# The first triple of each group sends its 264-column product ahead of the 272-column one

## The chip, the cores and the metric

The kernel runs on one core of one Trainium2 chip. The metric is the device time of one launch in microseconds (us), the median over runs. The engines are named as the profile names them: PE is TensorE (matrix products, with their weight loads as a stream of their own, PEld), DVE is VectorE, ACT is ScalarE, POOL is GpSimd and SP is SyncE, which issues the transfers.

## The reference, cut to what matters

One inference step of a one-layer hybrid decoder trunk. There are 264 tokens: 256 of a prompt and 8 of decode samples, each with 2048 features, all in float32.

```python
xn = rms_norm(x, g_mix)
z  = xn @ w_in                                   # 2048 -> 3584, split among three mixers
y_pool = pool_mixer(...) @ w_pool_br             #  512 -> 2048
y_lru  = (rg_lru(...) * gelu(u_gel)) @ w_lru_br  # 1024 -> 2048
y_conf = conformer(...) @ w_conf_br              #  512 -> 2048
gates  = sigmoid(xn @ w_gate + b_gate)           # 2048 -> 3 * 2048
x = x + (g_a*y_pool + g_b*y_lru + g_c*y_conf) @ w_out
hid = square(relu(rms_norm(x, g_mlp) @ w_up))    # 2048 -> 8192
x = x + hid @ w_down                             # 8192 -> 2048
y = rms_norm(x, g_final)
```

The states of the pooling, of the two convolutions and of the recurrence are outputs too. Nearly all of the work is the product of 264 tokens with weights that are read once.

## The kernel before, in words

*Three products for one.* TensorE takes float32 data rounded to a shorter form (fp32r), so each operand is split in a high part, the rounded value, and a low part, the rest. A product of x and w becomes hi(w)·hi(x) + lo(w)·hi(x) + hi(w)·lo(x), added up in PSUM. Here these three products are called a triple. On the activation side `high(t, k)` and `low(t, k)` lie next to each other in one row, low first: columns 0 to 263 are low, 264 to 527 are high, and in each the 256 prompt tokens come before the 8 samples. N is 264, TP is 256 and TS is 8.

*Two forms of a triple.* A form is three entries (low weights?, first column, last column). ALIKE sends three times 264 columns: high with whi, high with wlo, low with whi. MIXED sends 272, 264 and 256 columns: first the low part of the 8 samples together with the whole high part with whi (columns 256 to 527), then high with wlo, then low of the 256 prompt tokens with whi. The 8 sample columns of the first product go to their own place at the start of the PSUM bank (`ps[:, :8]`), and `join` or `add_side` adds them to the sample's columns when a group is evacuated. Both forms send 792 columns.

*Groups, chunks and order.* `weight_plan` (line 66) lists 67 groups, each one block of 512 output columns: 7 of w_in, 12 of w_gate, 4 each of w_pool_br, w_lru_br, w_conf_br and w_out, and 16 each of w_up and w_down. A group is cut into chunks, each with two rows of 128 weights (kt = 0, 1) and 512 columns, which are four tiles of 128 (m = 0 to 3). A chunk of 1024 columns is thus 8 triples, 24 products. A group of 2048 inputs has 8 chunks, one of 512 has 2. Each of the four tiles m adds up in its own PSUM bank (`acc`), and there are 8 banks, so two groups' worth. The first group (gi = 0) sends ALIKE, its first four chunks by operand and not by triple; all later groups send MIXED. Between them stand 4 chunks of the RG-LRU gates and one of the pooling's grouped map with 12 products of 264 columns each, and four single products with `ones_r` (line 323) for sums over features.

*What feeds TensorE.* SyncE reads the weights in the order of the plan into `raw`. For each chunk `split` (line 214) makes ScalarE round `raw` to `whi` (line 221), and VectorE subtract that from `raw` into `wlo` (line 222), three chunks ahead of the one that TensorE works on. The order on every queue is the order in which the program is written. `tile_mm` calls `mm3`, which calls `mm` (line 240) three times: every product of the three parts is recorded at line 243. The product that opens a bank has `start=True`. The evacuation of a group follows its last chunk, on VectorE for the most part, with background work of the mixers spread over the chunks by a table of costs (`run_bg`).

Of the kernel before, what the change touches and what calls it, by code (L numbers as in the profile page):

```python
# [91 lines left out]
def hybrid_step(ctx: ExitStack, tc: tile.TileContext, first, par_in, st_in, wall, y_out, st_out):  # L92
# [28 lines left out]
    def pv(name, i=None, n=1):  # L121
        a, b = PCOL[name]
        return par[:, a:b] if i is None else par[:, a + i:a + i + n]
# [26 lines left out]
    def acc():  # L150
        return psum.tile([P, 512], F32, name="acc", tag="acc")

    def tokens(ps):
        return ps[:, TS:TS + N]
# [22 lines left out]
    def dma_pair(p):  # L177
        s = (2 * p) % NRAW
        if p >= n_pairs:
            return  # L180
        if 2 * p >= SINGLE and chunks[2 * p][3] == chunks[2 * p + 1][3] == CH:
            nc.sync.dma_start(raw[:, s:s + 2, :], wall[p - FIRST // 2].rearrange("p (a c) -> p a c", a=2))
        else:
            for h in range(2):
                if chunks[2 * p + h][3]:
                    dma_part(2 * p + h, 0, chunks[2 * p + h][3])
# [27 lines left out]
    def split(j, half=None):  # L214
        if j >= len(chunks) or not chunks[j][3]:
            return
        r, h, lo = raw[:, j % NRAW, :], whi[:, j % NHI, :], wlo[:, j % NHI, :]
        s = slice(0, chunks[j][3])
        if half is not None:
            s = slice(half * 512, half * 512 + 512)  # L220
        nc.scalar.copy(h[:, s], r[:, s])  # L221
        nc.vector.tensor_tensor(lo[:, s], r[:, s], f(h[:, s]), op=ALU.subtract)  # L222
# [13 lines left out]

    ALIKE = (False, N, 2 * N), (True, N, 2 * N), (False, 0, N)
    MIXED = (False, TP, 2 * N), (True, N, 2 * N), (False, 0, TP)

    def mm(ps, hi, lo, x, what, start, stop=False):  # L240
        low_w, a, b = what
        o = TS + N - (b - a) if b > N else TS
        nc.tensor.matmul(ps[:, o:o + b - a], lo if low_w else hi, x[:, a:b], start=start, stop=stop,  # L243
                         skip_group_check=True)
# [119 lines left out]
    def x_tile(k):  # L364
        x_high(k)
        x_low(k)
# [31 lines left out]
    def softplus():  # L398
        sc = G[:, 8, :]
        t0, t1, t2, w, t4 = (sc[:, 8 * i:8 * i + 8] for i in range(5))  # L400
        lam = pv("lru_lambda")
        nc.scalar.activation(t0, lam, AF.Abs)
        nc.scalar.activation(w, t0, AF.Exp, scale=-1.0)
        nc.vector.tensor_scalar(t0, w, 2.0, None, op0=ALU.add)
        nc.vector.reciprocal(t1, t0)
        nc.vector.tensor_scalar(t4, lam, -1.0, 0.0, op0=ALU.mult, op1=ALU.max)
        eng = nc.gpsimd
        eng.tensor_tensor(t0, w, t1, op=ALU.mult)
        eng.tensor_tensor(t1, t0, t0, op=ALU.mult)
        terms = 10  # L410
        eng.memset(t2, 2.0 / (2 * terms + 1))
        for i in range(terms - 1, -1, -1):
            eng.tensor_tensor(t2, t2, t1, op=ALU.mult)
            eng.tensor_scalar(t2, t2, 1.0, 2.0 / (2 * i + 1), op0=ALU.mult, op1=ALU.add)
        eng.tensor_tensor(t2, t2, t0, op=ALU.mult)
        eng.tensor_tensor(t2, t2, t4, op=ALU.add)
        eng.tensor_scalar(sp[:, 0:8], t2, 4.0, 0.0, op0=ALU.mult, op1=ALU.add)
        eng.tensor_scalar(sp[:, 8:16], t2, -8.0, 0.0, op0=ALU.mult, op1=ALU.add)


    def small(at, n):
        return st[:, at - S_SMALL:at - S_SMALL + n]
# [7 lines left out]
    def state_move(i, move):  # L430
        move(tails[i], slice(i * TAIL, (i + 1) * TAIL))
# [481 lines left out]
    def group(gi):  # L913
        name, k0, _, m = groups[gi]
        if name == "w_in":
            def rhs(i):
                return both(a_all, i)
            fn = {0: pool_evac, 1: lru_x_copy, 2: lambda c, p: lru_x_evac(4 + c, p), 3: gel_evac,
                  4: lambda c, p: gel_evac(4 + c, p), 5: ca_evac, 6: cb_evac}[m]
            return rhs, fn  # L920
        if name == "w_gate":
            return (lambda i: both(a_all, i)), (lambda c, p: gate_evac(m // 4, m % 4, c, p))
        if name == "w_pool_br":
            assert "grp" in done
            return (lambda i: both(Q(), i)), (lambda c, p: branch_evac(0, m, c, p))
        if name == "w_lru_br":
            assert "lru" in done
            return (lambda i: both(LH(), i)), (lambda c, p: branch_evac(1, m, c, p))
        if name == "w_conf_br":
            assert "conf" in done  # L930
            return (lambda i: both(Q(), 4 + i)), (lambda c, p: branch_evac(2, m, c, p))
        if name == "w_out":
            return (lambda i: both(a_all, i)), (lambda c, p: out_evac(m * 4 + c, p))
        if name == "w_up":
            return (lambda i: both(*bpart(i))), (lambda c, p: up_evac(m // 4, (m % 4) * 4 + c, p))
        q = k0 // 16
        return (lambda i: both(*hid(q, i))), (lambda c, p: down_evac(q, m * 4 + c, p))
# [31 lines left out]

    def tile_mm(i, c, kt, m, rhs, pss, stop, form=MIXED):  # L970
        s = slice(kt * 512 + m * P, kt * 512 + (m + 1) * P)
        mm3(pss[m], whi[:, i % NHI, s], wlo[:, i % NHI, s], rhs(2 * c + kt), c == 0 and kt == 0, stop,
            form)
# [17 lines left out]
    for i, ch in enumerate(chunks):  # L991
        now[0] = i
        if i < 5:
            x_tile(2 * i + 6)
            x_tile(2 * i + 7)
        for half in (0, 1) if i < 2 else (None,):
            split(i + AHEAD, half)
        if i == 12:
            softplus()
            again = first[:, KD:KD + 4 * HEAD].rearrange("p (k c) -> p k c", k=4)[:, :, :N]  # L1000
            nc.sync.dma_start(X[:, 0:4, :], again)
            nc.vector.tensor_scalar(gfin, pv("g_final"), -0.5, None, op0=ALU.mult)
        if i % 2 == 0:
            dma_pair((i + 8) // 2)
        if i == 2:
            nc.sync.dma_start(par, par_in)
            nc.sync.dma_start(small(S_SMALL, S_IN - S_SMALL), st_in[:, S_SMALL:])
        if 13 <= i < 17:
            state_move(i - 13, lambda t, s: nc.sync.dma_start(t, st_in[:, s]))
        kind, gi, c, _ = ch  # L1010
        if kind == "dense":
            rhs, fn = group(gi)
            name = groups[gi][0]
            n = groups[gi][2] // 2
            if c == 0:
                pss = [acc() for _ in range(4)]
            if i < len(chunks) - 2:
                for kt in range(2):
                    if i < LEAD:
                        by_operand(i, kt, rhs, pss)  # L1020
                    for m in range(4 * (i < LEAD), 4):
                        tile_mm(i, c, kt, m, rhs, pss, c == n - 1 and kt == 1,
                                    MIXED if gi else ALIKE)
            elif i == len(chunks) - 1:
                for m in range(4):
                    for b in range(4):
                        tile_mm(i - 1 + b // 2, c - 1 + b // 2, b % 2, m, rhs, pss, b == 3)
            if c == n - 1:
                for m in range(4):
                    if (gi, m) == (len(groups) - 1, 3):  # L1030
                        last_evac(pss[m])
                    else:
                        if gi and name not in ("w_out", "w_down"):
                            join(pss[m], name in ("w_in", "w_conf_br"))
                        fn(m, pss[m] if name in ("w_out", "w_down") else tokens(pss[m]))
                after(gi)
        elif kind == "lru":
            for j in range(2):
                lru_gate_mm(2 * gi + j, i, j)
            if gi == 3:  # L1040
                lru_tail()
        elif kind == "grp":
            grp_mm(i)
        if i == len(chunks) - 4:
            nc.scalar.preload_act_table_set(ROOT)
        if 136 <= i < 140:
            state_move(i - 136, lambda t, s: nc.sync.dma_start(st_out[:, s], t))
        if i == 140:
            nc.sync.dma_start(st_out[:, S_SMALL:], st)
        if 5 <= i < 9:  # L1050
            x_squares(i - 5)
        if i == 9:
            later(0, x_sum)
        if i == 12:
            later(0, x_rms)
        run_bg()
# [148 lines left out]
```

## Time and profile before

| | |
|---|---|
| time, median of 3 runs | 1374.05 us (1373.83 to 1377.09) |
| the profiled execution | 1374.28 us, its span 1372.5 us |
| mean granted TensorE clock | 0.997 |
| busy: PE, DVE, ACT, POOL | 99%, 65%, 53%, 7% |
| instructions of PE | 11421 products, as many weight loads |
| read from device memory | 252.57 MB, 186 GB/s over the span |

How to read the rows that follow. A row of a group of instructions has line, engine, operation, output and inputs, shape and count, then the busy time and the mean duration in ns of one. Products are pipelined, and the ends that the profile gives them are modelled: one is shown as some 280 ns long while the next one starts about 119 ns later. So the pace of TensorE is read from starts, not from durations. A row of the timeline has start and length in us, and merges neighbours of the same name: a row with x2 is two products, the second of which started inside it. In such a row here, whi x2 is the last product of a triple and the first of the next, shown with the form of the first one. Each triple has one product with `wlo`, which has a row of its own.

### The profile page before, as it was taken

To read this page: it belongs to the slowest core of one execution; us is meant where nothing else is said; L and a number is where in the kernel's file an instruction comes from. 1 tells how busy PE (TensorE), PEld (TensorE's weight loads), DVE (VectorE), ACT (ScalarE), POOL (GpSimd) and SP (SyncE) were. 2 spreads that over 40 slices of the span, in tenths; PEclk is the share of its full clock that TensorE was granted. 3 is DMA by queue.
4 is the path that set the end of the run, shared out by engine and by line. 5 is a ranking of instruction groups with operands and counts; after the bars stand their busy time and mean duration, and the time that the engine had idled before them with its cause. 6 is when DMAs were issued, how large, how long until landed. Compare 5 with 4: busy or idle time off the path is not lost.

```text
span 1372.5 us, 26899 instructions
## 1 busy us (share of the span) xinstructions
PE 1362.0 (99%) x11421; PEld 1360.0 (99%) x11421; DVE 892.5 (65%) x1460; ACT 727.3 (53%) x1061; POOL 97.6 (7%) x125
## 2 busy tenths in 40 slices
PE   9999999999999999999999999999999999999997
PEld 9999999999999999999999999999999999999997
DVE  7686888876877669666656455655465645465544
ACT  7667677666664646455544334543344533354544
POOL 0230010110102014010000000000000000000013
PEclk9999999999999999999999999999999999999998
DMA  8655556555565555555555555555555555555552
GB/s 324 208 179 200 175 192 197 185 181 188 185 212 188 183 187 181 187 181 185 189 183 185 185 185 185 186 186 183 187 186 184 186 187 184 187 185 185 187 184 77
DMA packets 40824, 257.51 MB, mean 188 GB/s; under 512 B 4480, under 2 KB 6784, under 8 KB 11776
## 3 DMA queue, kind: packets, MB, share of 16 engines
q1 hardware_dynamic: 40272, 255.19, 54.8%
q8 instruction: 89, 1.46, 0.4%
q10 hardware_dynamic: 432, 0.61, 0.1%
q14 instruction: 31, 0.25, 0.1%
HBM read 252.57 MB, written 3.21 MB: 186 GB/s over the span
## 4 chain that ended last, share of the span: by engine, by line
PE 99%; DVE 0%; DMA 0%; ACT 0%; DVEq 0%; issue 0%
PE acc L243 99%; DMA tmp<-first_dram 0%; DVE y L1091 0%; DVE acc L1082 0%; DVEq L1182 0%; DVE G L1081 0%; DVE acc L1080 0%; PE acc L1068 0%; PE acc L323 0%; ACT whi L231 0%; ACT rstd L1075 0%; DVE G L892 0%; DVE X L889 0%; DVEq L1082 0%
## 5 line engine op out<-in xcount | busy, mean ns | idle before, releaser
L222 DVE TENSOR_TENSOR wlo<-raw,whi 128x1024 fp32r<-128x1024 f32 (+1 forms) x478 | 581.8, 1219 | 440.3 <-ACT whi L221 439.6
L221 ACT CAST whi<-raw 128x1024 fp32r<-128x1024 f32 (+1 forms) x478 | 496.9, 1042 | 569.8 <-PE acc L243 500.5
L243 PE MATMUL acc<-A,whi 128*128 128x256 f32 (+2 forms) x3968 | 709.3, 281 | 0.2 <-ACT whi L231 0.2
L243 PEld LDWEIGHTS acc<-A,whi 128*128 128x128 f32 x3968 | 609.4, 188 | 0.8 <-ACT whi L231 0.6
L243 PE MATMUL acc<-A,wlo 128*128 128x264 f32 x1984 | 555.3, 282 | 0.0
L243 PEld LDWEIGHTS acc<-A,wlo 128*128 128x128 f32 x1984 | 370.9, 188 | 0.0
L243 PE MATMUL acc<-xn,whi 128*128 128x272 f32 (+1 forms) x2048 | 366.0, 281 | 0.0
L243 PEld LDWEIGHTS acc<-xn,whi 128*128 128x128 f32 x2048 | 314.7, 188 | 0.0
L243 PE MATMUL acc<-xn,wlo 128*128 128x264 f32 x1024 | 288.5, 282 | 0.0
L243 PEld LDWEIGHTS acc<-xn,wlo 128*128 128x128 f32 x1024 | 192.2, 188 | 0.0
L243 PE MATMUL acc<-Q,whi 128*128 128x256 f32 (+2 forms) x776 | 140.7, 281 | 0.0
L243 PE MATMUL acc<-LH,whi 128*128 128x272 f32 (+1 forms) x768 | 138.9, 281 | 0.0
L243 PEld LDWEIGHTS acc<-Q,whi 128*128 128x128 f32 x776 | 120.1, 188 | 0.0
L243 PEld LDWEIGHTS acc<-LH,whi 128*128 128x128 f32 x768 | 118.7, 188 | 0.0
L243 PE MATMUL acc<-Q,wlo 128*128 128x264 f32 x388 | 109.3, 282 | 0.0
L243 PE MATMUL acc<-LH,wlo 128*128 128x264 f32 x384 | 108.2, 282 | 0.0
L860 POOL TENSOR_TENSOR G<-G 128x264 f32<-128x264 f32 x28 | 27.1, 968 | 789.0 <-ACT G L858 788.1
L243 PEld LDWEIGHTS acc<-Q,wlo 128*128 128x128 f32 x388 | 72.8, 188 | 0.0
L243 PEld LDWEIGHTS acc<-LH,wlo 128*128 128x128 f32 x384 | 72.1, 188 | 0.0
L640 ACT ACTIVATE G<-tmp,par 128x256 f32<-128x256 f32 x120 | 54.3, 500 | 7.9 <-DVE G L643 7.1
L643 DVE TENSOR_TENSOR G<-G 128x1024 f32<-128x1024 f32 x30 | 38.2, 1274 | 0.0
L899 DVE TENSOR_TENSOR X<-X,acc 128x264 f32<-128x264 f32 x79 | 33.4, 422 | 6.4 <-PE acc L243 6.4
(185 smaller groups left out, 591.3 us busy)
## 6 DMA issues: line engine op xcount, KB each, us to landing
raw<-wall_dram SPq DMA_DIRECT2D x226, 1024.0 KB, 4.9
raw<-wall_dram SPq DMA_DIRECT2D x12, 512.0 KB, 6.1
raw<-first_dram SPq DMA_DIRECT2D x6, 512.0 KB, 8.1
X<-first_dram SPq DMA_DIRECT2D x6, 264.0 KB, 7.7
raw<-wall_dram SPq DMA_DIRECT2D x5, 256.0 KB, 3.0
tmp<-first_dram SPq DMA_DIRECT2D x3, 388.0 KB, 4.5
y_dram<-y SPq DMA_DIRECT2D x3, 264.0 KB, 2.2
tmp<-st_dram SPq DMA_DIRECT2D x4, 188.0 KB, 5.1
```

The costliest lines, as they stand in the source:

```text
L221: nc.scalar.copy(h[:, s], r[:, s])
L222: nc.vector.tensor_tensor(lo[:, s], r[:, s], f(h[:, s]), op=ALU.subtract)
L243: nc.tensor.matmul(ps[:, o:o + b - a], lo if low_w else hi, x[:, a:b], start=start, stop=stop, skip_group_check=True)
L640: nc.scalar.activation(dst[:, ct, :TP], vext[:, ct, k:k + TP], AF.Copy, scale=par[:, w:w + 1])
L643: nc.vector.tensor_tensor(VC[:, :, :TP], VC[:, :, :TP], src[:, :, :TP], op=ALU.add)
L860: nc.gpsimd.tensor_tensor(sq2, sq2, t, op=ALU.add)
L899: nc.vector.tensor_tensor(X[:, m, :], X[:, m, :], tokens(whole), op=ALU.add)
```

## The change

In the first triple of every group but the first one (c = 0, kt = 0, m = 0), the first two products change places: high with wlo, 264 columns, opens the bank, and the 272-column product comes second. The third stays. The triples of the group's other three tiles, which open their banks as well, and all later triples keep the order 272, 264, 256.

```diff
     ALIKE = (False, N, 2 * N), (True, N, 2 * N), (False, 0, N)
     MIXED = (False, TP, 2 * N), (True, N, 2 * N), (False, 0, TP)
+    OPENING = MIXED[1], MIXED[0], MIXED[2]
...
                     for m in range(4 * (i < LEAD), 4):
                         tile_mm(i, c, kt, m, rhs, pss, c == n - 1 and kt == 1,
-                                    MIXED if gi else ALIKE)
+                                    ALIKE if not gi else MIXED if c or kt or m else OPENING)
```

## The prediction

> **What bounds the kernel now.** I read the page first (busy shares, chain), then the waits of TensorE, then the chain in order of time, then TensorE's groups with the forms kept apart, and last the timeline at single places.
>
> ```profile
> span 1372.5 us, 26899 instructions
> PE 1362.0 (99%) x11421; PEld 1360.0 (99%) x11421; DVE 892.5 (65%) x1460; ACT 727.3 (53%) x1061; POOL 97.6 (7%) x125
> PE acc L340 <- PEq L1176: 0.8, 1, 0.8
> PE acc L1068 <- DVE G L892: 0.3, 1, 0.3
> PE acc L243 <- ACT whi L231: 0.2, 1, 0.2
> 43.55 392.54 PE acc L243 x3300
> 436.21 22.83 PE acc L243 x192
> 459.17 85.63 PE acc L243 x720
> 647.93 713.35 PE acc L243 x6000
> ```
>
> The three rows with an arrow are all the waits of TensorE that this view has: 1.3 us in 1372.5. The last four are pieces of the chain that ended last (start, length, what, how many): it is nothing but the products of line 243, and the longest piece runs 6000 of them back to back. 713.35 / 6000 = 0.11889 us for a product, 0.3567 us for a triple of 272, 264 and 256 columns. So the kernel's time is the number of products times the pace at which TensorE takes them, and a change can act through a wait before a product, or through the pace. The piece of 6000 runs over 31 group boundaries without a break.
>
> The pace is not a property of the columns alone. Here are the rows of the products by form in three stretches (minimum, median and maximum ns of one, first and last start), single rows of TensorE's timeline, and three stretches from the windows, whose third figure from the end is the granted clock:
>
> ```profile
> L243 PE MATMUL acc<-A,wlo x34: 281/281/283, 16.8 to 28.4; 128*128 128x264 f32 x34
> L243 PE MATMUL acc<-A,whi x80: 283/285/288, 28.5 to 42.9; 128*128 128x272 f32 x40, 128*128 128x256 f32 x39, 128*128 128x264 f32 x1
> L243 PE MATMUL acc<-A,wlo x40: 281/286/286, 28.4 to 42.7; 128*128 128x264 f32 x40
> L243 PE MATMUL acc<-A,whi x456: 275/281/287, 547.8 to 629.0; 128*128 128x272 f32 x76, 128*128 128x256 f32 x76
> L243 PE MATMUL acc<-A,wlo x228: 281/282/283, 547.9 to 628.9; 128*128 128x264 f32 x114
> ...
> 16.83 0.40 PE L243 MATMUL acc<-A,wlo 128*128 128x264 f32 x2
> 17.20 0.28 PE L243 MATMUL acc<-A,wlo 128*128 128x264 f32 x1
> 28.36 0.28 PE L243 MATMUL acc<-A,wlo 128*128 128x264 f32 x1
> 28.72 0.29 PE L243 MATMUL acc<-A,wlo 128*128 128x264 f32 x1
> 42.65 0.29 PE L243 MATMUL acc<-A,wlo 128*128 128x264 f32 x1
> 43.26 0.29 PE L323 MATMUL acc<-L,ones_r 128*128 128x264 f32 x1
> 43.51 0.28 PE L243 MATMUL acc<-A,wlo 128*128 128x264 f32 x1
> 547.89 0.28 PE L243 MATMUL acc<-A,wlo 128*128 128x264 f32 x1
> 628.86 0.28 PE L243 MATMUL acc<-A,wlo 128*128 128x264 f32 x1
> ...
> 28.60:42.90 14.30, 14.30 (x120) 14.30 (x119) 12.45 (x17) 8.18 (x11) 0.00 (x0) 1.00 0.59 200
> 548.00:629.00 81.00, 81.00 (x684) 81.00 (x683) 50.37 (x73) 38.77 (x53) 9.29 (x11) 1.00 0.55 184
> 17.10:28.50 11.40, 11.40 (x98) 11.40 (x97) 8.48 (x11) 9.83 (x13) 0.00 (x0) 1.00 1.03 398
> ```
>
> There is one wlo product in each triple, so the step between them is the time of a triple.
> - Three times 264 columns (the first group): from 17.20 to 28.36 are 31 steps, 0.3600 us.
> - 272, 264, 256 in w_out: from 547.89 to 628.86 are 227 steps, 0.3567 us. I call this the quick pace.
> - The same 272, 264, 256 directly behind the first group: from 28.72 to 42.65 are 38 steps, 0.3666 us. The wlo product's median is 286 ns here against 282. I call this the slow pace. It held until one product of other operands, the ones product at 43.26, came in between.
>
> All three add up to 792 columns, with the granted clock at 1.00 in each. So the stream of weight loads and products locks into one pace or another, by what came before, and stays there. This is the only thing in the profile through which an exchange of two neighbouring products can be worth more than itself.
>
> **The change part by part.** The list of instructions that the changed kernel builds, against that of before, differs in 66 places on TensorE: in the first triple of each of the 66 groups behind the first, the 264-column product with wlo now stands ahead of the 272-column product with whi. VectorE, ScalarE, GpSimd and SyncE issue the same instructions in the same order with the same waits. Nothing is added or removed: as many products, weight loads, columns and PSUM writes as before.
>
> *The wait that moves.* The wlo product waits for VectorE's subtraction and now stands one product, 0.12 us, earlier; behind it, in TensorE's queue, is the whole stream. The group with the least slack opens at 97.6, the usual one has that of 721.96:
>
> ```profile
> 95.28 1.22 DVE L222 TENSOR_TENSOR wlo<-raw,whi 128x1024 fp32r<-128x1024 f32 x1
> 97.72 0.28 PE L243 MATMUL acc<-A,wlo 128*128 128x264 f32 x1
> 714.68 1.22 DVE L222 TENSOR_TENSOR wlo<-raw,whi 128x1024 fp32r<-128x1024 f32 x1 [1.63 <-ACT whi L221]
> 721.96 0.28 PE L243 MATMUL acc<-A,whi 128*128 128x272 f32 x1
> 722.08 0.28 PE L243 MATMUL acc<-A,wlo 128*128 128x264 f32 x1
> ```
>
> The residue is ready at 95.28 + 1.22 = 96.50 and at 715.90, 1.22 and 6.18 us ahead of the product that reads it. Moving it 0.12 us up leaves 1.1 us at the tightest place, so this costs 0; the cover is the three chunks by which the splits run ahead. If the cover were gone everywhere, it would cost one product per group, 66 × 0.12 = 7.9 us. The whi product is now wanted later, which frees nothing: no opening waited for it. The last product of the triple, and with it each release of a weight buffer or of PSUM, keeps its place, so no cast, split, evacuation or transfer is started at another time.
>
> *The order itself.* Before has a 264 behind a 256 only where products of other operands come in, and never a 256 behind a 272, so the direct cost has to be bounded. Nearest are the chain's pieces. Behind a ones product: 22.83 − 64 × 0.3567 = 0.00 us over a piece of 64 triples, and 85.63 − 240 × 0.3567 = 0.02 us over one of 240. The piece of 3300 has five blocks of 264-column products in it, 60 products in all (the four lru gate blocks and one grouped map of 12 each; the rows of whi stand in the last fence, x32 and x8, and each has half as many of wlo): 392.54 − 1080 × 0.3567 − 20 × 0.3600 = 0.1 us, 0.02 for each block. That is what it costs to throw the stream out of step once and let it find the quick pace again. On the other side an opening could be a little shorter: neighbouring starts in the timeline lie 0.11 to 0.13 us apart, so 0.01 us is what one product could win. Per opening −0.01 to +0.03 us, over 66: −0.7 to +2.0 us. I take +0.01, the middle of the two pieces behind a ones product, since one product out of place is nearest to what an exchange does: +0.7 us.
>
> *The sum.* The profiled execution took 1374.28 us (a span of 1372.5 and 1.8 around it): 1374.28 + 0 + 0.7 = 1375.0. The median of the runs, 1374.05, is 0.2 lower, so I forecast 1374.8 us, with 1373.3 to 1376.1 as this case's own range. Faster or slower by 0.3% (4.1 us) is about what a measurement of this kernel can tell from no change.
>
> [...]
>
> **The rivals.**
>
> *Slower: an opening throws the stream into the slow pace, and it stays.* Price: 0.3666 − 0.3567 = 0.0099 us a triple. The triples are those of
>
> ```profile
> L243 PE MATMUL acc<-A,whi 128*128 128x272 f32 x1920 | 547.4, 285 | 0.0
> L243 PE MATMUL acc<-xn,whi 128*128 128x272 f32 x1024 | 291.8, 285 | 0.0
> L243 PE MATMUL acc<-Q,whi 128*128 128x272 f32 x384 | 109.4, 285 | 0.0
> L243 PE MATMUL acc<-LH,whi 128*128 128x272 f32 x384 | 109.4, 285 | 0.0
> ...
> L243 PE MATMUL acc<-L,whi 128*128 128x264 f32 x32 | 6.5, 284 | 0.0
> L243 PE MATMUL acc<-Q,whi 128*128 128x264 f32 x8 | 1.6, 284 | 0.0
> ```
>
> The first four rows make 1920 + 1024 + 384 + 384 = 3712, of which 40 are slow already. All the others: 3672 × 0.0099 = 36 us, 1411 us; half of them (one opening locks it, the next unlocks it): 1392 us. It decides over the sign as soon as 4.1 / 0.0099 = 414 triples, 11%, go slow. For it: the pace exists, held 39 triples with no wait behind it, and began at a group opening. Against it: in the rest of the trace the stream was disturbed ten times (four blocks of lru gates, one grouped map, four ones products, that at 43.26 among them, and one short stall in w_out) and each time it came to the quick pace, at the prices worked out above.
>
> *Faster: an opening finds a quicker pace than any seen.* The three paces lie 3.3 ns (360.0 − 356.7) and twice that (366.6 − 360.0) apart. One such step below the quick one, an estimate from these rows, is 353.4 ns: 3712 × 0.0033 = 12 us, 1362 us. For it: the paces do come in steps, and nothing shows that the quick one is the lowest. Against it: no stretch of 1372 us shows it.
>
> *The wlo wait takes over:* 1374.3 + 7.9 = 1382 us at most. The slack of 1.1 us at the tightest opening speaks against it.
>
> That the change doesn't do what it says is out: the built list shows the 66 exchanges.
>
> **How the numbers follow.** Eleven times the stream was thrown out of step: once it locked slow. The same opening recurs, so its outcome is not averaged over 66 tries but repeats for a kind of boundary. With five kinds (A to A, into Q, into LH, back to A, into xn2), each with 10 in 11 for quick, all stay quick with (10/11)^5 = 0.62, so slow 0.38. A quicker pace was met 0 times in 11; I give it 0.20 all the same, since none of the eleven was an exchange of lengths. The wait gets 0.01, and no change keeps 0.41. Faster 0.20, same 0.41, slower 0.39. The range reaches over the slow case, down to 1371 for the spread of the runs, up to 1411; it leaves out the quicker pace and little else.
>
> **What would show it.** Right: TensorE's chain in pieces of 0.1189 us a product, the wlo product's median at 282 ns after the openings, no new wait on VectorE's wlo, 1.3 us of TensorE waits. Slow pace: wlo steps of 0.3666, whi products with a minimum of 283 instead of 275, the span longer with TensorE still at 99% and no wait. Quicker pace: wlo steps under 0.3567 and a shorter span. Moved wait: TensorE waiting on L222 at group starts. What would make me wrong is that I cannot compute which pace an opening leads to; I only count.

## The result, and the profile after

The changed kernel took 1390.76 us (median of 4 runs, 1390.45 to 1391.04) against 1375.57 us (1373.83 to 1377.34) for the kernel before beside it: a ratio of 1.011, with a 95% interval of 1.0093 to 1.0128. It is slower by some 15 us. That is not the forecast of 1374.8 us; it lies within 1.3 us of the rival's second sum, the slow pace in half of the triples (1392 us). Two of the four runs of the kernel before are some 3 us longer than the other two (1377.09 and 1377.34 against 1373.83 and 1374.05); against the two shorter ones the loss is 16.8 us.

The profiled execution took 1390.54 us. Here are the span and the busy shares from its page, all waits of TensorE, and the pieces of the chain that ended last (start, length, what, count):

```profile
span 1388.8 us, 26900 instructions
PE 1378.3 (99%) x11421; PEld 1376.5 (99%) x11421; DVE 892.4 (64%) x1460; ACT 725.8 (52%) x1061; POOL 97.3 (7%) x125
...
PE acc L341 <- PEq L1177: 0.8, 1, 0.8
PE acc L1069 <- DVE G L893: 0.3, 1, 0.3
PE acc L244 <- ACT whi L231: 0.2, 1, 0.2
...
42.87 397.64 PE acc L244 x3300
440.63 22.84 PE acc L244 x192
463.59 190.70 PE acc L244 x1584
654.42 723.16 PE acc L244 x6000
```

The span is 16.3 us longer (1388.8 against 1372.5). Nothing waits more: the three waits are the same 1.3 us as before, TensorE is at 99% again, and the same 6000 products that took 713.35 us now take 723.16, in one piece without a break. The whole loss is pace. (The line that records the products is 244 now; it was 243.)

Two neighbouring groups of w_up show it. First the products of group 37 by form, then those of group 38 (minimum, median and maximum ns of one, first and last start), then rows of TensorE's timeline at the openings of the groups 36 to 40 (start, length):

```profile
L244 PE MATMUL acc<-xn,whi x128: 279/285/288, 682.7 to 705.9; 128*128 128x256 f32 x64, 128*128 128x272 f32 x64
L244 PE MATMUL acc<-xn,wlo x64: 282/286/286, 682.8 to 706.0; 128*128 128x264 f32 x64
...
L244 PE MATMUL acc<-xn,whi x128: 275/283/288, 706.1 to 728.7; 128*128 128x256 f32 x64, 128*128 128x272 f32 x64
L244 PE MATMUL acc<-xn,wlo x64: 281/282/292, 706.3 to 728.9; 128*128 128x264 f32 x64
...
659.86 0.28 PE L244 MATMUL acc<-xn,whi 128*128 128x256 f32 x1
659.97 0.28 PE L244 MATMUL acc<-xn,wlo 128*128 128x264 f32 x1
682.68 0.28 PE L244 MATMUL acc<-xn,whi 128*128 128x256 f32 x1
682.80 0.28 PE L244 MATMUL acc<-xn,wlo 128*128 128x264 f32 x1
706.14 0.28 PE L244 MATMUL acc<-xn,whi 128*128 128x256 f32 x1
706.26 0.29 PE L244 MATMUL acc<-xn,wlo 128*128 128x264 f32 x1
729.11 0.28 PE L244 MATMUL acc<-A,wlo 128*128 128x264 f32 x1
752.57 0.29 PE L244 MATMUL acc<-A,wlo 128*128 128x264 f32 x1
```

The wlo medians of 286 and 282 ns are those of the slow and the quick pace in the prediction. From opening to opening, group 36 takes 22.83 us, group 37 23.46, group 38 22.85, group 39 23.46: 64 triples at 0.3567 or at 0.3666. So one opening locks the slow pace, and the next one unlocks it.

Over the whole trace, with each of the 3712 triples taken from its own first start to the next product's, 1653 run slow (365 to 369 ns) and 1957 quick (356 to 360), where before it was 42 and 3658. (1653 − 42) × 0.0099 = 15.9 us of the 16.3. Most of the rest lies at the openings: the triples that are neither went from 12 to 102.

**What decides an opening.** In the quick stream the triples are not all alike. The time from the start of a triple's 256-column product to the start of what follows is 112 or 113 ns in one triple and 117 or 118 in the next, and so on in turn (113, 117, 113, 118 ns ahead of the opening at 682.80); in the slow stream it is 119 or 120 in every triple. Sorted by that time in front of the exchanged triple, from the starts in ns (all openings behind the first one that is exchanged):

```
pace before -> behind   openings   gap behind the 256-column product
quick -> quick              4      113 ns (4)
quick -> slow              31      117 ns (13), 118 ns (18)
slow  -> quick             30      119 ns (23), 120 ns (7)
```

There is no exception. An exchange behind a short gap keeps the quick pace; behind a long gap it locks the slow one; in the slow stream it releases it. In the rows above it is 0.11 at 659.86 (stays quick), 0.12 at 682.68 (locks); these rows are rounded to 0.01 us, and a single one does not always show it. A group has an even number of triples, so the alternation comes through a whole group in step. This was read from the same trace that it explains, so it had to be tested.

### The profile page after: what moved, and what is told of

The parts are those of the page before. It is cut to its first block, busy times and chain, and to the rows that moved or that the text cites. A ratio compares the mean times of both kernels' runs of the same rounds, so it can differ in the third digit from the quotient of the medians.

```text
span 1388.8 us, 26900 instructions
## 1 busy us (share of the span) xinstructions
PE 1378.3 (99%) x11421; PEld 1376.5 (99%) x11421; DVE 892.4 (64%) x1460; ACT 725.8 (52%) x1061; POOL 97.3 (7%) x125
## 4 chain that ended last, share of the span: by engine, by line
PE 99%; DVE 0%; DMA 0%; ACT 0%; DVEq 0%; issue 0%
PE acc L244 99%; DMA tmp<-first_dram 0%; DVE y L1092 0%; DVE acc L1083 0%; DVEq L1183 0%; DVE G L1082 0%; DVE acc L1081 0%; PE acc L1069 0%; PE acc L324 0%; ACT whi L231 0%; ACT rstd L1076 0%; DVE G L893 0%; DVE X L890 0%; DVEq L1083 0%
## 5 line engine op out<-in xcount | busy, mean ns | idle before, releaser
L244 PE MATMUL acc<-xn,whi 128*128 128x272 f32 (+1 forms) x2048 | 370.1, 283 | 0.0
```

## The experiments

All the runs below are compared with runs of the kernel before on the same chip, 1373.95 us (19 runs), 1374.22 (13) or 1374.12 (21) in the median.

### One, two and three exchanges

The exchange is made at group 37 alone, at 37 and 38, and at 37, 38 and 39. If each exchange had its own price, two would cost twice what one does. By the alternation, one costs nothing but shifts the step, the second locks the pace for all 29 groups that follow, and the third releases it.

```diff
-ALIKE if not gi else MIXED if c or kt or m else OPENING)
+ALIKE if not gi else OPENING if gi == 37 and not (c or kt or m) else MIXED)               # one
+ALIKE if not gi else OPENING if gi in (37, 38) and not (c or kt or m) else MIXED)         # two
+ALIKE if not gi else OPENING if gi in (37, 38, 39) and not (c or kt or m) else MIXED)     # three
```

> The exchange in one group alone, group 37 (the third of w_up), all others as before. Theory of the lock: in the quick stream the triples come in two kinds that alternate, seen in the gap behind the 256-column product (112 to 113 ns, then 117 to 118). In the changed kernel an exchange behind a triple with the 117 to 118 ns gap led to the slow pace, one behind the 112 to 113 ns gap kept the quick one and shifted the alternation by one triple. In the kernel before, group 37 opens behind a short gap, so here nothing locks: no more than 0.1 us slower than before. Rival, a toll: each exchange costs its share of what 66 cost, 15.2 / 66 = 0.23 us. Rival, any exchange in the quick stream locks slow: the 1920 triples from there to the end at 9.9 ns, +19 us.

> The exchange in groups 37 and 38 alone. Theory of the lock: the first shifts the alternation, so that the second falls behind the long gap and locks the stream slow; no exchange follows to set it free, and nothing else comes in between until the end: 29 groups with 64 triples at 9.9 ns, +18.4 us, about 1392.5 us. Two exchanges would then cost more than the 66 of the changed kernel. Toll: 2 x 0.23 = 0.5 us.

> The exchange in groups 37, 38 and 39 alone. Theory of the lock: shift, lock, release; only the 64 triples of group 38 are slow, +0.6 us, and the rest of the chain has the pace of before. Toll: 3 x 0.23 = 0.7 us, so the time doesn't tell these two apart, but the trace does: 64 slow triples in group 38 and none behind it.

One: 1373.82 us, ratio 1.0 (0.9991 to 1.0009). Two: 1393.9 us, 1.0143 (1.0126 to 1.016). Three: 1374.85 us, 1.0 (0.9987 to 1.0013). The last piece of the chain and the openings in the timeline; of one:

```profile
647.45 713.38 PE acc L244 x6000
675.74 0.28 PE L244 MATMUL acc<-xn,whi 128*128 128x256 f32 x1
675.85 0.28 PE L244 MATMUL acc<-xn,wlo 128*128 128x264 f32 x1
```

of two:

```profile
647.76 731.91 PE acc L244 x6000
676.02 0.28 PE L244 MATMUL acc<-xn,whi 128*128 128x256 f32 x1
676.13 0.28 PE L244 MATMUL acc<-xn,wlo 128*128 128x264 f32 x1
698.85 0.28 PE L244 MATMUL acc<-xn,whi 128*128 128x256 f32 x1
698.97 0.28 PE L244 MATMUL acc<-xn,wlo 128*128 128x264 f32 x1
```

and of three:

```profile
544.99 105.84 PE acc L244 x864
650.82 0.12 PE acc L324
650.95 714.01 PE acc L244 x6000
```

The exchange at 37 stands behind a gap of 0.11 and changes nothing (713.38 against 713.35); that at 38, behind 0.12, costs 731.91 − 713.38 = 18.5 us (29 groups × 64 triples × 0.0099 = 18.4), although it exchanges just two products; the third leaves group 38 alone slow, 0.63 us. Two exchanges cost more than 66, and three cost next to nothing. No price for each exchange can do that; a pace that an opening locks and the next one unlocks does.

Three shows something else besides. Its profiled run was one of 1377.92 us. The kernel before, too, has runs of 1376 to 1377.3 us beside those of 1373 to 1375, 14 of 57 in this study, and one more of 1379.36. In the row at 544.99, 864 products behind the short stall in w_out took 105.84 us, where the profile of before has

```profile
544.83 102.97 PE acc L243 x864
```

The difference is 2.87 us, and 288 triples × 0.0099 are 2.85. The pace locked slow behind the stall, and the ones product at 650.82 released it. No exchange lies in that stretch. The stall is in the profile of before too, and there the stream came out of it quick.

The slow stretch behind the first group is no fixed one either. In the profiles of before, one and two its 39 triples are slow; in that of three they are quick from the third on, though group 1 is sent alike in all four.

### The exchange in the middle of a group

An opening also starts a PSUM bank and a group. Here the two exchanges are made in the fifth chunk of the groups 37 and 38, where neither starts.

```diff
-ALIKE if not gi else MIXED if c or kt or m else OPENING)
+ALIKE if not gi else OPENING if gi in (37, 38) and (c, kt, m) == (4, 0, 0) else MIXED)
```

> The exchange in groups 37 and 38 again, but in the first triple of their fifth chunk and not in the first triple of the group: there the product that comes first opens no bank, it adds to what is there. Theory of the lock: where in a group it stands doesn't matter; the fifth chunk starts an even number of triples (32) behind the group's start, so as with the exchanges at the openings the second locks: 1856 - 32 = 1824 triples, +18.1 us. Rival, the opening of a bank with 264 columns in place of 272 is what disturbs: no effect, 1374 us.

1393.43 us, ratio 1.0135 (1.0113 to 1.0157). The last piece of the chain is

```profile
647.45 731.59 PE acc L244 x6000
```

18.2 us over that of one, 0.3 less than in two, which is the half group that now comes ahead of the lock. The opening as such has no part in it.

### Columns or weights

The exchange moves two things: 264 columns come ahead of 272, and wlo comes ahead of whi. In the first kernel only the columns change places and whi stays first; in the second only the weights do.

```diff
-    OPENING = MIXED[1], MIXED[0], MIXED[2]
+    OPENING = (False, N, 2 * N), (True, TP, 2 * N), (False, 0, TP)      # lengths alone
+    OPENING = (True, TP, 2 * N), (False, N, 2 * N), (False, 0, TP)      # weights alone
-ALIKE if not gi else MIXED if c or kt or m else OPENING)
+ALIKE if not gi else OPENING if gi in (37, 38) and not (c or kt or m) else MIXED)
```

> In the opening triples of groups 37 and 38 only the columns are exchanged, not the weights: 264 columns with whi, 272 with wlo, 256 with whi (the low part of the 8 sample columns is thus multiplied with the low weights there, and its product with the high weights is left out). If the lengths and places of the columns make the lock, the same as the two exchanges: +18 us, about 1393 us, slow from group 38 on. If it is the order of the weights, no change, 1374 us.

> The counterpart: in the opening triples of groups 37 and 38 the weights are exchanged, not the columns: 272 columns with wlo, 264 with whi, 256 with whi (the same part left out). If the columns make the lock: no change, 1374 us, the last piece of the chain 713.4 us as before. If the order of the weights does: +18 us.

Lengths alone: 1392.57 us, ratio 1.0132 (1.0112 to 1.0152). Weights alone: 1373.75 us, 0.9997 (0.9987 to 1.0007). The last pieces, of lengths alone and then of weights alone:

```profile
648.09 731.91 PE acc L244 x6000
```

```profile
647.35 713.35 PE acc L244 x6000
```

The exchange of the columns alone gives the whole effect, 731.91 us as in two. The test of the weights is weaker than it looks. Their exchange at 37 did not shift the alternation, so that at 38 also fell behind a short gap (113 and 112 ns in front of the two), where even the whole exchange locks nothing. It shows that the weights alone do not shift the step; an exchange of weights alone behind a long gap was not run. The columns have a length and a place of their own (each product reads another part of the row of activations), and these two were not told apart.

### The new order in every triple

```diff
-ALIKE if not gi else MIXED if c or kt or m else OPENING)
+ALIKE if not gi else OPENING if True else MIXED)
```

> All triples behind the first group send 264, 272, 256 columns, not the openings alone. The three products then follow each other in the one other order that a cycle of three has. Theory of the lock: no opening shifts the alternation any more, so the pace is one and the same over long pieces, whichever it is: 1374 us if this order can run at 356.7 ns a triple, 1411 us if it runs at 366.6 throughout; a value between them, with groups in turn quick and slow as in the changed kernel, would be against it. I have nothing that tells which; a toll for each exchange would give 3712 x 0.23 = 854 us more.

1410.15 us, ratio 1.0259 (1.0242 to 1.0277); the last piece is

```profile
663.91 733.20 PE acc L244 x6000
```

733.20 / 2000 = 0.3666 us for a triple: the slow pace. The order 264, 272, 256 showed no quick stretch in this run. The 16 triples of the last two chunks are sent by a line of their own and keep the old order; the last 12 of them are back at 0.3567. The prediction's upper end, every triple slow at 1411 us, is what this kernel runs at.

### The place of the activations in a row

If the pace hangs on how three reads of a row follow each other, it may hang on where they start. Each row of a stored activation begins at the column `k * PITCH + SKEW`, with `SKEW = 56`; 4 columns are 16 bytes. The kernel before is moved as a whole.

```diff
-SKEW = 56
+SKEW = 64      # and 60, and 72
```

> The kernel before with SKEW 64 in place of 56: every row of the activations' two parts starts 32 bytes later, so that the low part starts at a multiple of 64 bytes in place of the high part. The products' lengths and order are those of before. If the paces are a matter of the lengths alone, 1374 us. If they are a matter of where the columns lie, the piece of 6000 products leaves its 713.4 us; whether up or down I can't say.

> The kernel before with SKEW 60 in place of 56: all rows of the activations start 16 bytes later. With 64 (32 bytes later) the stream ran at 360.0 and 373.3 ns a triple in place of 356.7 and 366.6. If what counts is the place within 64 bytes, this is a third set of paces; if only the step of 32 bytes counts, one of the two known ones. The last piece of 6000 products tells: 713.4 us at 356.7 ns, 720.0 at 360.0.

> The kernel before with SKEW 72, 64 bytes later than 56: the same place within 64 bytes, another one within 128. If the place within 64 bytes makes the paces, all is as before: 713.4 us for the last 6000 products, 1374 us. If a longer period counts, another pace.

With 60: 1396.69 us, ratio 1.0163 (1.0144 to 1.0181). With 72: 1397.72 us, 1.017 (1.0152 to 1.0189). With 64: 1394.68 in the run with the profile and 1417.40 to 1418.34 in the three others, so no ratio is given. The last pieces for 60, 64 and 72, each from its own chain:

```profile
656.77 726.68 PE acc L243 x6000
```

```profile
661.69 720.02 PE acc L243 x6000
```

```profile
658.04 726.68 PE acc L243 x6000
```

That is 0.3633, 0.3600 and 0.3633 us a triple, where 56 has 0.3567. Not one product, weight or column is exchanged here, and the pace moves by up to 1.9%. If the place within 64 bytes made the pace, 72 would run like 56; it does not, and that reading fell.

The kernel with 64 has two paces as well. Of an earlier piece of 64 triples its profile says

```profile
443.57 23.88 PE acc L243 x192
```

That is 0.3731 us a triple, against 0.3600 in the last piece. What took the three longer runs of 64 to 1418 us was not profiled; a long stretch in the slower of these paces would be a way, and is not shown.

### Without the stall, and the best of both

The locking behind the stall in w_out (three, above) can be taken away at its cause. The two background steps that cast and subtract an operand of w_out were two chunks apart; here the subtraction comes one chunk earlier. The second kernel adds the exchange at group 1 alone: in the changed kernel the slow pace that follows the first group, 39 triples in the profile of before, ended after 3.

```diff
-            later_split(A(k), A(16 + k), t, 3, 2)
+            later_split(A(k), A(16 + k), t, 3, 1)
# best, in addition:
-ALIKE if not gi else MIXED if c or kt or m else OPENING)
+ALIKE if not gi else OPENING if gi == 1 and not (c or kt or m) else MIXED)
```

> The kernel before, with the low parts of the merged branches split one chunk earlier on VectorE (gap 1 in place of 2 in later_split), so that the third chunk of w_out finds them ready. In the profile of the run with three exchanges the same short stall in w_out was followed by the slow pace up to the ones product at 650, and its piece of 864 products took 105.84 us in place of 102.97. Theory of the lock: with the stall gone the stream stays quick there in every run, the piece takes 864 / 3 x 0.3567 = 102.7 us, and the runs at 1376 to 1377.5 us that the kernel before has beside those at 1374 are gone: all at 1373.3 to 1374.3. Rival, the stall only costs itself: 0.25 us less in every run, and the two kinds of run stay.

> The same, and the exchange at the opening of the second group (group 1) alone, where the kernel before runs 39 triples slow and the changed kernel found the quick pace after three. Theory of the lock: group 1 quick, 36 x 9.9 ns = 0.36 us less than without the exchange; nothing later changes, since the ones product in that group sets the stream quick anyway. About 1373.3 us; a difference of 0.03% that the time hardly tells, and the trace does.

Without the stall: 1373.49 us (11 runs, 1373.04 to 1374.36), ratio 0.9993 (0.9984 to 1.0002). Best: 1373.11 us (11 runs, 1372.79 to 1373.89), the same ratio and interval. The chain without the stall, and that of best:

```profile
4.55 37.88 PE acc L243 x312
458.17 188.36 PE acc L243 x1584
646.65 713.38 PE acc L243 x6000
```

```profile
4.51 37.73 PE acc L244 x312
458.00 188.35 PE acc L244 x1584
646.48 713.38 PE acc L244 x6000
```

The stall is gone: 1584 products in one piece of 188.36 us where the kernel before has two of 85.63 and 102.97. None of these 22 runs took more than 1374.36, while 4 of the 21 of the kernel before beside them took 1376.3 to 1377.1; that fits the stall as the source of the longer runs, though 22 runs are few. What the exchange at group 1 is worth stays open: without it, too, the profile shows group 1 quick from its third triple on, and the first 312 products differ by 0.15 us (37.88 and 37.73). The gain in the median, 0.6 and 1.0 us, is below what these runs can tell from none.

## Why the prediction was right or wrong

- **What bounds the kernel: right.** The time is the products times their pace; TensorE is at 99% in both kernels, with no new wait.
- **The wait that moves: right.** 0 was taken; TensorE's waits are the same three rows, 1.3 us, and none is on the subtraction that makes `wlo`.
- **The direct cost of the order: right in size, and small.** Within −0.01 to +0.03 us: an exchanged triple took 0.359 us where the quick pace stays, 0.362 where it locks, and 0.370 with 0.361 behind it where it releases, against 0.3567. That the mean over the openings, 0.011, lies so near the +0.01 that was taken is luck: that was borrowed from pieces behind a ones product, which are another thing.
- **The sum failed in one step: that the stream finds the quick pace again.** It was taken from ten of eleven disturbances, as a chance for each kind of boundary. Both halves of that are wrong. The outcome does not repeat for a kind of boundary: the groups 36, 37 and 38 open the same way, from xn2 to xn2, and the first stays quick, the second locks, the third releases. And it is no chance: it goes by the phase of the alternation in which the exchange falls. The ten disturbances were blocks of other products, single ones products and a stall; none of them was an exchange of columns in a running stream, so their count said little about this one. Nor is the count itself fixed: behind the first group and behind the stall the stream came out slow in one profile and quick in another, with the same products there (before and three). What could have been read in the trace of before is the alternation of 112 and 117 ns behind the 256-column products, which I did not look at: it shows that equal triples of the quick stream come in two phases, though not yet what an exchange does in each. The measured time lies inside the stated 1371 to 1411 us because that range was drawn over the rival; the sum's own range, 1373.3 to 1376.1, misses it by 14.7.
- **The price of the slow pace: right.** 0.0099 us a triple, from 39 triples in the first 43 us, held for the 1653 slow triples here, for the 1856 of two, and for those in the new order everywhere. The rival's sentence "one opening locks it, the next unlocks it" was one of two sums for it, and is what happens; 1392 us was the sum, 1390.76 the median. I had no row that told which of the two it would be, so that the second sum came so near is in part luck: that nearly every second opening locked follows from the alternation and the even number of triples in a group, which the sum did not use.
- **The quicker pace: not seen.** No triple pace below 0.3567 us turned up in any of these kernels.
- **What the columns alone would give: not what is measured.** The Trainium skill, "TensorE: Matmul & The Clock Gate", Back-to-back issue gap, gives columns / 2.4 GHz + 2.5 ns as the gap of an isolated warm product, and says that in a stream of weight loads and products both of them set the spacing. For 792 columns in three products the first would be 337.5 ns, an estimate from that page. Each product here has its weight load, and the triples take 356.7 or 366.6 ns, for equal columns and at the same granted clock of 0.997. How much of the difference from 337.5 is due to the weight loads no run here shows.

The mechanism is shown as far as this: two paces with one price, locked and released by the order of the columns alone, without any change of the weights or the opening of a bank or group, by the phase that the exchange meets, and with a pace that depends also on where the reads start. What inside TensorE, or in the memory it reads from, makes the gaps alternate stays open; no run here looks inside.

## What to carry to other kernels

When an engine is busy 99% and waits for nothing, its pace is still to be checked: take the step between the starts of equal products in several stretches, and if two values occur for the same work, look for what switches them before anything in the order is touched. In the profiles of all these kernels TensorE was 99% busy, had waits of at most 1.8 us in all and a granted clock of 0.997 or 0.998, while the time went from 1373 to over 1410 us. A small edit to such a stream is to be tried at one, two and three places: a cost that doesn't grow with their number is a state, not a price.

## What was not expected of the hardware

- One exchange of two neighbouring products changes the pace of the 1856 triples that follow it: 18.5 us, while the products exchanged cost 0.02 us at most themselves (0.370 + 0.361 − 2 × 0.3567).
- In the quick stream equal triples alternate, 112 to 113 ns and 117 to 118 ns behind the 256-column product, and which of the two an exchange meets decided all 35 openings that came in the quick pace.
- Moving all activations in their rows costs, over the last 6000 products, 13.3 us for 16 bytes (726.68 − 713.38), 6.6 for 32 (720.02 − 713.38) and 13.3 again for 64.
- The slow pace can lock behind a short stall as well: 2.87 us more in the stretch behind that of w_out, with no exchange in it. It did so in the profile of three and not in those of before and one, which have the same stall and the same products.
